# The beginning of an FFN in another order: the forms of x and the first pair's fetch beside the second chunk, a plain unit in front of the first pair

## The chip, the cores and the metric

The kernel runs on one core of a Trainium2 chip. The metric is the device time of one execution in microseconds; it was 1357.7 us, the median of three runs (1357.37 to 1358.7). The engines are PE (TensorE, the matrix products), DVE (VectorE), ACT (ScalarE), POOL (GpSimd) and SP (SyncE, which issues nearly all DMAs). Each engine works through its own instructions in the order in which they were issued, and waits on semaphores for the others.

## The reference

Two layers of a decoder trunk on 256 tokens of width 1024, in float32. Each layer has two gated feed-forward networks (FFNs), a mixer between them and an embedding gate behind them, so there are four FFNs in the program:

```
h = h + 0.5 * SwiGLU_a(RMSNorm(h))
h = h + mixer(RMSNorm(h))
h = h + 0.5 * SwiGLU_b(RMSNorm(h))
h = h + sigmoid(RMSNorm(h) @ W_pg) * (p[i] @ W_pe)
swiglu(x, w1, w3, w2) = (silu(x @ w1) * (x @ w3)) @ w2        # 1024 -> 2816 -> 1024
```

Only the beginning of each FFN is touched by the change, and what is computed stays the same.

## The kernel before

**Products.** Float32 is worked with in two parts: every weight tile and every tile of x is split into a high part (a cast, on ACT, into `whi`, `q` or `xhi`) and the rest (a subtraction, on DVE, into `wlo`, `q` or `xlo`). `mm3` (L102 to L104) forms a product from three matmuls, high by high, high by low, low by high. x holds two token blocks (tb 0 and 1) of 128 tokens, in eight slices (kt) of 128 columns.

**Loads.** `load` (L85 to L87) fetches a tile of 128x1024 (512 KB) into one of four `raw` buffers and splits it. `split_w` splits a tile `wr` that lies in SBUF already (through L135 on ACT and L136 on DVE).

**Chunks, units and pairs.** The hidden width is worked in 11 chunks of 256 columns. Chunk c of w1 and w3 together is four units of 512 KB. A *plain* chunk is 48 matmuls (`up`, or unit by unit `up_unit`, in block lists `("P", c, i)`); `gated` then takes its two banks of PSUM, by `act` on ACT (L236) and `pr` on DVE (L238), to the gated hidden values. `turn` transposes these (L250) for the second product, and `("D", c, j)` is a unit of it, into four banks `acc`. Chunks 5 to 10 are done in *pairs*, by seven products of half size in place of eight (a Winograd form of Strassen's scheme), in the order 1, 2, 5, 3, 6, 7, 4. Each pair fetches four quarters x, y, w and z of the weights, two tiles each (L326), forms sums of them (L330 on DVE; one is an accumulating DMA from POOL, L334), splits them (`make`), and multiplies them with forms of x. Products 1 and 2 use the columns of x as they stand; products 5, 3, 6, 7 and 4 use `q` tiles that `x_forms` makes (L267 to L311): the second token block is rescaled by the quotient of the two row scales, which a matmul with a matrix of ones spreads over the partitions (L274), copied by ACT (L276) and multiplied in by DVE (L297); sums and differences follow (L284, L293, L305), and five splits.

**Order.** The program is written out engine by engine by a tile scheduler that takes the instructions in about the order of the code, and lets an engine's instruction go earlier where its buffers allow. The order around the change is the code's own: chunk 0, chunk 1, then the forms of x, the first pair's fetch, the transposes of chunk 0, and then a block list that starts with "S", a step of the pair: the next `make`, the next sum of quarters, and one product. The first FFN (`first`) differs in what stands beside it: x comes from DRAM in parts, h and the constants are loaded between the units, and chunk 1 goes into the banks `acc`.

The names that the prediction uses: `pr` (L238), the forms' product L274, the adds L293, the scaling L297, the subtractions L284, the last sum L305, the fetch L326, the sum of quarters L330, and the splits by L86/L87 (raw tiles) and L135/L136 (all others).

Of the kernel before, what the change touches and what calls it, by code (L numbers as in the profile page):

```python
# [14 lines left out]
P = 128  # L15
L = 2
S = 256
TB = S // P
D = 1024
# [14 lines left out]
def trunk(ctx: ExitStack, tc: tile.TileContext, a: dict, out: bass.AP):  # L34
# [14 lines left out]
    def const(name, shape):  # L49
        t = cp.tile(shape, F32, tag=name, name=name)  # L50
        tc.keep_in_program_order(nc.sync.dma_start(t, a[name]))
        return t
# [62 lines left out]
    def bank_acc():  # L115
        return bank("acc", 4)
# [74 lines left out]
    def ffn(li, w13, w2, r, g, first=False, aside=None):  # L191
        nonlocal ident
        with tc.tile_pool(name=nm("fp"), bufs=3) as fp:
# [7 lines left out]
            if first:  # L201
                un0 = start(wtile)
            acc = []
            ffT = {}
            prs = {}

            def up(c, un, bank):
                os = []
                for tb in range(TB):
                    o = bank()  # L210
                    for kt in range(KT):
                        w = [x[:, (kt % 2) * 512 : (kt % 2) * 512 + 512] for x in un[kt // 2]]
                        mm3(o, x_at(tb, kt), w, kt == 0, kt == KT - 1)
                        if kt == 1:
                            settle()
                    os.append(o)
                    if r is not None:
                        gated(c, tb, o, r[tb])
                return os


# [12 lines left out]
            def gated(c, tb, o, scale):  # L234
                act = fp.tile([P, FC], F32, tag="act", name=nm("act"), bufs=2)
                A.activation(act, o[:, :FC], AF.Silu, scale=scale)  # L236
                pr = fp.tile([P, FC], F32, tag="pr", name=nm("pr"), bufs=6)
                V.scalar_tensor_tensor(  # L238
                    out=pr, in0=o[:, FC:], scalar=scale, in1=act, op0=ALU.mult, op1=ALU.mult
                )  # L240
                prs[c, tb] = pr
# [189 lines left out]
                        turn(*arg)  # L431
                return following

            for c in range(2):
                if first and c == 1:

                    un = []
                    for i in range(4):
                        un.append(load(w13[li, c, i]))
                        if i < 2:  # L440
                            load_h(i)
                    ident = const("ident", [P, P])
                    r = [norm_r(tb) for tb in range(TB)]
                    for tb, o in enumerate(os0):
                        gated(0, tb, o, r[tb])
                    up(c, un, bank_acc)
                else:
                    os0 = up(c, un0 if first and c == 0 else [load(w13[li, c, i]) for i in range(4)], bank_mm)
                if c == 1:
                    acc.extend(bank_acc() for _ in range(4))  # L450
                    fx = x_forms()
                    wg = pair(5, bank_tr)
                    for q in "xywz":
                        wg[1](q)
                if c >= 1:
                    turn(c - 1)
            wg[0](1)
            if first:
                later()
            wg = block(wg, [  # L460
                ("S",), ("P", 2, 0), ("D", 0, 0), ("S",), ("P", 2, 1), ("S",), ("D", 0, 1), ("P", 2, 2), ("S",),
                ("T", 1), ("P", 2, 3), ("S",), ("D", 1, 0), ("S",), ("D", 1, 1), ("S",), ("T", 2),
            ], (7, bank_tr))
            wg = block(wg, [
# [14 lines left out]
            un = {(c, j): load(w2[li, 2 * c + j]) for c in (9, 10) for j in range(2)}  # L479
# [561 lines left out]
    def load_h(tb):  # L1041
        tc.keep_in_program_order(nc.sync.dma_start(h[tb], a["x"][tb * P : (tb + 1) * P, :]))
# [7 lines left out]
    ident = gmla = gsub = ropec = ropes = lamv = maskm = biasd = masks = tri = None  # L1050
    r = None
# [93 lines left out]
```

## Time and profile before

| | us |
| --- | --- |
| median of three runs | 1357.7 (1357.37 to 1358.7) |
| the profiled execution | 1355.51 |
| its span | 1353.7 |
| its mean granted PE clock | 0.985 of full speed |
| beginnings of the four FFNs (chunk 1 ends) at about | 29, 479, 699, 1150 |

The profiled execution is one execution under the hardware profiler; its rows are given from the span's start, which lies 1.8 us inside the execution. A row of the timeline gives the start, the duration, the engine, the line of the kernel, the operation with output and inputs, and the shape; in brackets stands how long the engine was idle before it and what ended that. Matmuls overlap, so their pace is read from start to start and not from the duration. A row of a window gives, for each engine, the busy time and the number of instructions in that stretch, and behind them the granted clock of PE, the share of the DMA engines' time in use, and their rate.

### The profile page before, as it was taken

What the parts mean: (1) busy time and instruction counts of PE and PEld (TensorE: products, weight loads), DVE (VectorE), ACT (ScalarE), POOL (GpSimd) and SP (SyncE); (2) the same over time, 40 slices, a digit from 0 to 9 for tenths busy, and PEclk for the clock granted to TensorE, in tenths of its full rate; (3) what the DMA queues carried; (4) which work ended last, traced back from release to release, by engine and by line L of the source; (5) the groups of instructions that cost most, each with busy time, mean ns of one, the idle gap of its engine ahead of it and who ended that gap; (6) DMA issues with size and microseconds to landing.
All of it is one profiled execution on the core that took longest, in us unless ns stands there. A gap on an engine that the chain in (4) does not pass through costs nothing.

```text
span 1353.7 us, 18041 instructions
## 1 busy us (share of the span) xinstructions
PE 1308.6 (97%) x6576; PEld 1093.2 (81%) x6576; DVE 1042.0 (77%) x1466; ACT 837.2 (62%) x1257; POOL 69.5 (5%) x133
## 2 busy tenths in 40 slices
PE   8899999999999979999979999999999999799997
PEld 6688889978888858888858888898888788688886
DVE  6998875666768689897769988666666675998875
ACT  5666556665775456665746666566667744666655
POOL 1000000001100000000100000000010000000000
PEclk9899999999999989999999999999999999899999
DMA  8975457433546568555568744473444466675552
GB/s 306 314 251 156 139 164 222 167 125 126 169 143 186 190 211 276 187 147 180 170 219 273 234 121 150 147 225 134 156 145 136 157 187 241 210 236 160 155 169 81
DMA packets 71225, 249.21 MB, mean 184 GB/s; under 512 B 8544, under 2 KB 9184, under 8 KB 71136
## 3 DMA queue, kind: packets, MB, share of 16 engines
q1 hardware_dynamic: 67104, 234.39, 51.1%
q0 software_dynamic: 3456, 12.58, 5.5%
q8 instruction: 51, 0.84, 0.2%
q10 hardware_dynamic: 576, 1.08, 0.2%
q14 instruction: 38, 0.31, 0.1%
HBM read 246.98 MB, written 1.05 MB: 183 GB/s over the span
## 4 chain that ended last, share of the span: by engine, by line
PE 91%; DVE 5%; issue 1%; ACT 1%; DMA 1%; SPq 0%; POOLq 0%; POOL 0%; ACTq 0%
PE mm L102 15%; PE mm L104 14%; PE mm L103 14%; PE acc L103 8%; PE acc L104 8%; PE acc L102 8%; PE tr L103 6%; PE tr L102 5%; PE tr L104 5%; PE tr L250 1%; PE tr L150 1%; DVE q L136 1%; DVE wlo L136 1%; PE tr L742 1%; DVE wlo L87 1%
## 5 line engine op out<-in xcount | busy, mean ns | idle before, releaser
L87 DVE TENSOR_TENSOR wlo<-raw,whi 128x1024 fp32r<-128x1024 f32 (+1 forms) x346 | 411.4, 1200 | 93.1 <-ACT whi L86 90.8
L86 ACT CAST whi<-raw 128x1024 fp32r<-128x1024 f32 (+1 forms) x346 | 354.3, 1033 | 165.7 <-PE acc L104 52.3
L102 PE MATMUL mm<-whi,xhi 128*128 128x512 f32 (+1 forms) x632 | 247.1, 396 | 0.0
L104 PE MATMUL mm<-whi,xlo 128*128 128x512 f32 (+1 forms) x632 | 245.8, 389 | 0.0
L103 PE MATMUL mm<-wlo,xhi 128*128 128x512 f32 (+1 forms) x632 | 245.6, 389 | 0.0
L135 ACT CAST whi<-wr 128x1024 fp32r<-128x1024 f32 (+1 forms) x176 | 179.9, 1032 | 93.2 <-PE acc L104 53.1
L136 DVE TENSOR_TENSOR wlo<-wr,whi 128x1024 fp32r<-128x1024 f32 (+1 forms) x176 | 207.4, 1198 | 25.7 <-ACT whi L135 24.5
L104 PEld LDWEIGHTS mm<-whi,xlo 128*128 128x128 f32 x632 | 118.7, 188 | 24.8 <-DVE xlo L136 0.7
L102 PEld LDWEIGHTS mm<-whi,xhi 128*128 128x128 f32 x632 | 118.7, 188 | 24.4 <-DVE sqk L542 0.7
L104 PE MATMUL acc<-whi,flo 128*128 128x512 f32 x352 | 137.6, 391 | 0.0
L103 PEld LDWEIGHTS mm<-wlo,xhi 128*128 128x128 f32 x632 | 118.9, 188 | 23.1 <-DVE wlo L136 0.2
L103 PE MATMUL acc<-wlo,fhi 128*128 128x512 f32 x352 | 137.1, 390 | 0.0
L102 PE MATMUL acc<-whi,fhi 128*128 128x512 f32 x352 | 135.2, 392 | 0.0
L102 PE MATMUL tr<-whi,q 128*128 128x512 f32 x240 | 94.1, 392 | 0.0
L104 PE MATMUL tr<-whi,q 128*128 128x512 f32 x240 | 93.6, 390 | 0.0
L103 PE MATMUL tr<-wlo,q 128*128 128x512 f32 x240 | 93.4, 389 | 0.0
L330 DVE TENSOR_TENSOR wr<-wr,wr 128x1024 f32<-128x1024 f32 x72 | 86.3, 1222 | 0.0
L104 PEld LDWEIGHTS acc<-whi,flo 128*128 128x128 f32 x352 | 66.1, 188 | 13.8
L103 PEld LDWEIGHTS acc<-wlo,fhi 128*128 128x128 f32 x352 | 66.1, 188 | 13.5
L102 PEld LDWEIGHTS acc<-whi,fhi 128*128 128x128 f32 x352 | 66.1, 188 | 13.4
L102 PE MATMUL tr<-whi,xhi 128*128 128x512 f32 x96 | 42.3, 440 | 33.0 <-ACT whi L135 32.3
L102 PE MATMUL mm<-xhi,whi 128*128 128x256 f32 x256 | 73.8, 288 | 0.0
(253 smaller groups left out, 2169.0 us busy)
## 6 DMA issues: line engine op xcount, KB each, us to landing
wr<-in_w13a SPq DMA_DIRECT2D x48, 512.0 KB, 6.2
raw<-in_wg SPq DMA_DIRECT2D x48, 512.0 KB, 3.8
wr<-in_w13b SPq DMA_DIRECT2D x48, 512.0 KB, 5.8
raw<-in_w2a SPq DMA_DIRECT2D x44, 512.0 KB, 4.4
raw<-in_w2b SPq DMA_DIRECT2D x44, 512.0 KB, 4.3
raw<-in_w13b SPq DMA_DIRECT2D x40, 512.0 KB, 4.3
raw<-in_w13a SPq DMA_DIRECT2D x36, 512.0 KB, 4.6
raw<-in_wqk SPq DMA_DIRECT2D x32, 512.0 KB, 3.8
```

Of the source, the lines that this page charges most:

```text
L86: A.copy(hi[:, c], raw[:, c])
L87: V.tensor_tensor(out=lo[:, c], in0=raw[:, c], in1=hi[:, c].bitcast(F32), op=ALU.subtract)
L102: PE.matmul(o, lhs[0], rhs[0], start=first, stop=False, **more)
L103: PE.matmul(o, lhs[0], rhs[1], start=False, stop=False, **more)
L104: PE.matmul(o, lhs[1], rhs[0], start=False, stop=last, **more)
L135: A.copy(hi, t)
L136: V.tensor_tensor(out=lo, in0=t, in1=hi.bitcast(F32), op=ALU.subtract)
L150: PE.transpose(t[:, j * P : (j + 1) * P], h[tb][:, k * P : (k + 1) * P], ident)
L250: PE.transpose(t[:, j * S + tb * P : j * S + (tb + 1) * P], prs[c, tb][:, j * P : (j + 1) * P], ident)
L330: V.tensor_tensor(out=t[q][u], in0=t[q][u], in1=t[other][u], op=ALU.add)
L742: PE.transpose(t[:, j * P : (j + 1) * P], e[:, j * P : (j + 1) * P], ident)
```

## The change

`up` takes a function that it calls after the first token block. The loop over chunks 0 and 1 is written out: the forms of x (`begin`) are issued ahead of chunk 1's products (in the first FFN between its two token blocks); the first pair's quarters x, y and w are issued between chunk 1's units (in the first FFN behind them), z behind chunk 1; and the first block list begins with the plain unit `("P", 2, 0)` and not with a step of the pair. Because of two added lines, all lines behind `up` have numbers that are two higher: L274 is L276, L293 is L295, L297 is L299, L284 is L286, L305 is L307, L326 is L328, L330 is L332, L238 is L240, L250 is L252.

```diff
-            def up(c, un, bank):
+            def up(c, un, bank, then=None):
                 os = []
                 for tb in range(TB):
...
                     if r is not None:
                         gated(c, tb, o, r[tb])
+                    if tb == 0 and then is not None:
+                        then()
                 return os
...
-            for c in range(2):
-                if first and c == 1:
-
-                    un = []
-                    for i in range(4):
-                        un.append(load(w13[li, c, i]))
-                        if i < 2:
-                            load_h(i)
-                    ident = const("ident", [P, P])
-                    r = [norm_r(tb) for tb in range(TB)]
-                    for tb, o in enumerate(os0):
-                        gated(0, tb, o, r[tb])
-                    up(c, un, bank_acc)
-                else:
-                    os0 = up(c, un0 if first and c == 0 else [load(w13[li, c, i]) for i in range(4)], bank_mm)
-                if c == 1:
-                    acc.extend(bank_acc() for _ in range(4))
-                    fx = x_forms()
-                    wg = pair(5, bank_tr)
-                    for q in "xywz":
-                        wg[1](q)
-                if c >= 1:
-                    turn(c - 1)
+            def begin():
+                nonlocal fx
+                fx = x_forms()
+
+
+            fx = None
+            os0 = up(0, un0 if first else [load(w13[li, 0, i]) for i in range(4)], bank_mm)
+            wg = pair(5, bank_tr)
+            un = []
+            for i in range(4):
+                un.append(load(w13[li, 1, i]))
+                if first and i < 2:
+                    load_h(i)
+                if not first and i > 0:
+                    wg[1]("xyw"[i - 1])
+            if first:
+
+                ident = const("ident", [P, P])
+                r = [norm_r(tb) for tb in range(TB)]
+                for tb, o in enumerate(os0):
+                    gated(0, tb, o, r[tb])
+                for q in "xyw":
+                    wg[1](q)
+                up(1, un, bank_acc, begin)
+            else:
+                begin()
+                up(1, un, bank_mm)
+            wg[1]("z")
+            acc.extend(bank_acc() for _ in range(4))
+            turn(0)
             wg[0](1)
             if first:
                 later()
             wg = block(wg, [
-                ("S",), ("P", 2, 0), ("D", 0, 0), ("S",), ("P", 2, 1), ("S",), ("D", 0, 1), ("P", 2, 2), ("S",),
+                ("P", 2, 0), ("S",), ("D", 0, 0), ("S",), ("P", 2, 1), ("S",), ("D", 0, 1), ("P", 2, 2), ("S",),
                 ("T", 1), ("P", 2, 3), ("S",), ("D", 1, 0), ("S",), ("D", 1, 1), ("S",), ("T", 2),
             ], (7, bank_tr))
```

How it moves instructions is seen at three places. The first is PE in the second FFN, around the end of chunk 1; `mm_4624` is chunk 1's second bank, `tr_4742` product 1's. Before:

```order
L102 MATMUL mm_4624<-whi_4590,xhi 128x512
L103 MATMUL mm_4624<-wlo_4591,xhi 128x512
L104 MATMUL mm_4624<-whi_4590,xlo 128x512
L274 MATMUL tr_4662<-xg_4660,ones 128x128
L250 MATMUL tr_4717<-ident,pr_4540 128x128 x2
L250 MATMUL tr_4717<-ident,pr_4569 128x128 x2
L102 MATMUL tr_4742<-whi_4724,xhi 128x512 [waits Activation_49]
L103 MATMUL tr_4742<-wlo_4725,xhi 128x512 [waits DVE_49]
```

And now, from the end of chunk 1 (`mm_4680`) on, with `mm_4738` and `mm_4739` the banks of the plain unit and `tr_4762` that of product 1:

```order
L104 MATMUL mm_4680<-whi_4602,xlo 128x512
L252 MATMUL tr_4717<-ident,pr_4540 128x128 x2
L252 MATMUL tr_4717<-ident,pr_4569 128x128 x2
L102 MATMUL mm_4738<-whi_4733,xhi 128x512 [waits DVE_49]
L103 MATMUL mm_4738<-wlo_4734,xhi 128x512
L104 MATMUL mm_4738<-whi_4733,xlo 128x512
...
L102 MATMUL tr_4762<-whi_4724,xhi 128x512
L103 MATMUL tr_4762<-wlo_4725,xhi 128x512
L104 MATMUL tr_4762<-whi_4724,xlo 128x512
L102 MATMUL tr_4762<-whi_4724,xhi 128x512
L102 MATMUL mm_4739<-whi_4733,xhi 128x512 [waits DVE_49]
L103 MATMUL mm_4739<-wlo_4734,xhi 128x512
```

The product with the ones has left this place: it now stands ahead of chunk 1's 48 matmuls, as L276. Behind the transposes come the plain unit's matmuls for the first token block, four matmuls of product 1, and then those for the second block, whose bank is freed by a `pr`.

The second place is DVE in the second FFN, from the last split of chunk 1's weights on. Before, the two `pr` of chunk 1 (`pr_4622` and `pr_4651`) stood ahead of the forms:

```order
L238 SCALAR_TENSOR_TENSOR pr_4622<-mm_4595,r_4406,act_4620 128x256
L238 SCALAR_TENSOR_TENSOR pr_4651<-mm_4624,r_4461,act_4649 128x256
L297 TENSOR_TENSOR wr_4666<-wr_4666,rb_4664 128x512 x2
L136 TENSOR_TENSOR flo_4716<-tr_4717,fhi_4715 128x512
L284 TENSOR_TENSOR wr_4668<-wr_4666 128x512
...
L136 TENSOR_TENSOR q_4696<-wr_4666,q_4695 128x512
L136 TENSOR_TENSOR wlo_4725<-wr_4699,whi_4724 128x1024
L136 TENSOR_TENSOR wlo_4729<-wr_4700,whi_4728 128x1024
L136 TENSOR_TENSOR wlo_4733<-wr_4701,whi_4732 128x1024
```

Now, where `pr_4569` belongs to chunk 0 and `pr_4678` and `pr_4707` to chunk 1:

```order
L136 TENSOR_TENSOR wlo_4725<-wr_4571,whi_4724 128x1024
L136 TENSOR_TENSOR wlo_4729<-wr_4572,whi_4728 128x1024
L240 SCALAR_TENSOR_TENSOR pr_4569<-mm_4542,r_4461,act_4567 128x256
L299 TENSOR_TENSOR wr_4618<-wr_4618,rb_4616 128x512 x2
L87 TENSOR_TENSOR wlo_4734<-raw_4732,whi_4733 128x1024
...
L240 SCALAR_TENSOR_TENSOR pr_4678<-mm_4651,r_4406,act_4676 128x256
L307 TENSOR_TENSOR wr_4619<-wr_4619,wr_4620 128x512
L136 TENSOR_TENSOR wlo_4753<-wr_4573,whi_4752 128x1024
...
L136 TENSOR_TENSOR wlo_4757<-wr_4574,whi_4756 128x1024
L240 SCALAR_TENSOR_TENSOR pr_4707<-mm_4680,r_4461,act_4705 128x256
L136 TENSOR_TENSOR flo_4716<-tr_4717,fhi_4715 128x512
```

The splits of quarter x (`wlo_4725`, `wlo_4729`) have moved ahead of chunk 0's second `pr`, and the forms, the splits of y and the plain unit's split now stand between the `pr` of chunk 0 and the last `pr` of chunk 1.

The third place is DVE in the first FFN, from chunk 1's last `pr` on (`pr_372`, which was `pr_316`):

```order
L136 TENSOR_TENSOR wlo_390<-wr_202,whi_389 128x1024
L136 TENSOR_TENSOR wlo_394<-wr_203,whi_393 128x1024
L240 SCALAR_TENSOR_TENSOR pr_301<-acc_274,r_247,act_299 128x256
L240 SCALAR_TENSOR_TENSOR pr_372<-acc_345,r_258,act_370 128x256
L295 TENSOR_TENSOR wr_312<-xhi,xlo 128x512 x2
L299 TENSOR_TENSOR wr_312<-wr_312,rb_310 128x512 x2
L295 TENSOR_TENSOR wr_313<-xhi,xlo 128x512 x2
L286 TENSOR_TENSOR wr_314<-wr_312 128x512
L136 TENSOR_TENSOR flo_381<-tr_382,fhi_380 128x512
L286 TENSOR_TENSOR wr_312<-wr_313,wr_312 128x512
L136 TENSOR_TENSOR q_323<-wr_314,q_322 128x512
L87 TENSOR_TENSOR wlo_419<-raw_417,whi_418 128x1024
```

Here the forms follow chunk 1 as they did before; quarter x is split ahead of them, the four adds L295 have come in from a place far ahead, and the plain unit's split (`wlo_419`) stands behind six of the forms' instructions and `flo`.

## The prediction

> **What bounds the kernel now.** I read the page's first part, then TensorE's waits, then the stretches around the largest of them, then their rows.
>
> ```profile
> span 1353.7 us, 18041 instructions
> PE 1308.6 (97%) x6576; PEld 1093.2 (81%) x6576; DVE 1042.0 (77%) x1466; ACT 837.2 (62%) x1257; POOL 69.5 (5%) x133
> ```
>
> TensorE (PE) is busy for 97% of the span, so an order can win back only the time in which PE stands, or runs at a lower clock. Its waits, grouped (engine, line, releaser: us in total, times, longest):
>
> ```profile
> PE tr L102 <- ACT whi L135: 32.3, 4, 8.1
> PE tr L103 <- DVE wlo L136: 1.9, 4, 0.5
> ```
>
> That is four stalls of 8.1 + 0.5 us, one at each FFN's beginning: 34.2 of the 45.1 us in which PE is not busy. The stretches around the first two (busy us of PE, PEld, DVE, ACT, POOL; granted clock, DMA share, GB/s):
>
> ```profile
> 20.00:30.00 10.00, 8.99 (x41) 6.67 (x39) 4.33 (x9) 4.95 (x12) 1.01 (x3) 1.00 0.61 198
> 30.00:40.00 10.00, 1.60 (x3) 1.00 (x4) 9.89 (x15) 6.33 (x10) 0.00 (x0) 0.66 1.02 396
> 40.00:50.00 10.00, 10.00 (x38) 8.05 (x38) 10.00 (x10) 7.36 (x9) 1.93 (x2) 0.83 0.97 262
> ...
> 460.00:470.00 10.00, 10.00 (x45) 8.28 (x45) 8.32 (x15) 4.93 (x7) 0.05 (x1) 1.00 0.60 178
> 470.00:480.00 10.00, 10.00 (x48) 8.28 (x46) 0.48 (x1) 0.94 (x3) 0.00 (x0) 1.00 1.01 404
> 480.00:490.00 10.00, 1.44 (x4) 0.78 (x3) 9.85 (x15) 6.30 (x12) 0.00 (x0) 0.68 0.36 127
> ```
>
> In the second FFN VectorE (DVE) rests for 9.5 of the ten microseconds before the stall and works for 9.85 of the ten in which PE stands; and the clock falls meanwhile. PE's rows there (start, us, line, operation, idle before and its releaser):
>
> ```profile
> 478.87 0.39 PE L103 MATMUL mm<-wlo,xhi 128*128 128x512 f32 x1
> 479.10 0.40 PE L104 MATMUL mm<-whi,xlo 128*128 128x512 f32 x1
> 479.33 0.39 PE L274 MATMUL tr<-xg,ones 128*128 128x128 f32 x2
> 479.56 0.60 PE L250 MATMUL tr<-ident,pr 128*128 128x128 f32 x4
> 488.24 0.79 PE L102 MATMUL tr<-whi,xhi 128*128 128x512 f32 x1 [8.09 <-ACT whi L135]
> 489.50 0.79 PE L103 MATMUL tr<-wlo,xhi 128*128 128x512 f32 x1 [0.47 <-DVE wlo L136]
> ...
> 493.08 0.63 PE L102 MATMUL tr<-whi,xhi 128*128 128x512 f32 x1
> 493.51 0.59 PE L103 MATMUL tr<-wlo,xhi 128*128 128x512 f32 x1
> 493.93 0.39 PE L104 MATMUL tr<-whi,xlo 128*128 128x512 f32 x1
> ```
>
> L274, the product that the forms of x wait for, stands behind chunk 1, at 479.33. A matmul takes 0.23 us from start to start before the stall and 0.43 us behind it, until 493.93. DVE's rows:
>
> ```profile
> 468.56 0.69 DVE L136 TENSOR_TENSOR pT<-xg,pT 128x512 fp32r<-128x512 f32 x1 [1.28 <-ACT pT L135]
> 469.22 0.48 DVE L238 SCALAR_TENSOR_TENSOR pr<-mm,r,act 128x256 f32<-128x256 f32 x1
> 474.60 0.48 DVE L238 SCALAR_TENSOR_TENSOR pr<-mm,r,act 128x256 f32<-128x256 f32 x1 [4.90 <-ACT act L236]
> 480.04 0.48 DVE L238 SCALAR_TENSOR_TENSOR pr<-mm,r,act 128x256 f32<-128x256 f32 x1 [4.96 <-ACT act L236]
> 480.44 1.28 DVE L297 TENSOR_TENSOR wr<-wr,rb 128x512 f32<-128x512 f32 x2
> ...
> 485.72 2.50 DVE L136 TENSOR_TENSOR q<-wr,q 128x512 fp32r<-128x512 f32 x4
> 488.23 4.63 DVE L136 TENSOR_TENSOR wlo<-wr,whi 128x1024 fp32r<-128x1024 f32 x4
> 492.77 2.36 DVE L330 TENSOR_TENSOR wr<-wr,wr 128x1024 f32<-128x1024 f32 x2
> ```
>
> From 480.44 to 488.23 DVE makes the forms (7.8 us), and only then splits the first pair's quarter x, which product 1 needs. Product 1 uses plain x: it waits for the order alone.
>
> **What the change removes.** L274 (now L276) goes ahead of chunk 1, and in FFNs 2 to 4 the splits of quarter x and most of the forms run while PE works through chunk 1. The cover for 7.8 us of forms and 2.3 us for the two splits of x is the 9.5 us in which DVE rests; what does not fit ends behind chunk 1 and is counted below. What PE wins in FFN 2: from the stall's beginning (488.24 - 8.09 = 480.15) to the return of the clock (493.93) pass 13.78 us, with 11 matmuls in them, worth 11 x 0.2275 = 2.50: 11.3 us. The other FFNs by the same sum:
>
> ```profile
> 37.94 0.80 PE L102 MATMUL tr<-whi,xhi 128*128 128x512 f32 x1 [8.09 <-ACT whi L135]
> 43.51 0.39 PE L104 MATMUL tr<-whi,xlo 128*128 128x512 f32 x1
> ...
> 708.36 0.80 PE L102 MATMUL tr<-whi,xhi 128*128 128x512 f32 x1 [8.08 <-ACT whi L135]
> 712.60 0.39 PE L104 MATMUL tr<-whi,xlo 128*128 128x512 f32 x1
> ...
> 1158.29 0.80 PE L102 MATMUL tr<-whi,xhi 128*128 128x512 f32 x1 [8.08 <-ACT whi L135]
> 1163.05 0.40 PE L102 MATMUL tr<-whi,xhi 128*128 128x512 f32 x1
> ```
>
> FFN 1: 43.51 - 29.85 less 11 matmuls, 11.2. FFN 3: 712.60 - 700.28 less 8, 10.5. FFN 4: 1163.05 - 1150.21 less 9, 10.8. At most, then, 43.8 us.
>
> The Trainium skill (TensorE: Matmul & The Clock Gate, Part 1) says that the array falls to half clock after an idle window of about 3.4 us, and comes back after about as long a busy one, with windows that run freely. By its figure a stall costs at most some 1.7 us of lost clock, an estimate; the rows of FFN 2 give 11.3 - 8.6 = 2.7, FFN 3 only 1.9. FFN 4 gives 2.3. By the page the gain of these three would be some 1.8 us less in sum; the rows decide here.
>
> **What it adds.** The plain unit P 2,0 now comes first, six matmuls for each token block, in two banks that chunk 1 has just used. The second block's matmuls need the bank that the last `pr` (before at 480.04) reads out, and on DVE this `pr` now has the forms ahead of it. I count from the end of chunk 1's last split, 468.56 - 1.28 = 467.3, with 1.15 us for 1024 elements (4.63/4), 0.62 for 512 (2.50/4), 0.45 for a `pr`: two splits of x 2.3; `pr` 0.45; two L299 1.24; the unit's split 1.15; three L286 1.86; an L332 1.15; `pr` 0.45; L307 0.62; two splits of y 2.3; five of q 3.1. That is 14.6 us, so the last `pr` begins at 481.9 and ends at 482.4. PE comes to this place at about 479.3 + 0.2 (transposes) + 6 x 0.2275 + 4 x 0.2275 (product 1's first) = 481.8. A wait of 0.6 us if nothing lands late. Below stands nothing, above two splits that wait for their data, 2.5. I take 0.9, since chunk 1's last unit now stands behind quarters on the queue. Behind the waiting matmul stand eight of product 1, the rest of whose operands are ready, and nothing on another engine needs them sooner.
>
> DVE keeps pace afterwards: before, it has done all that stands up to L330 x2 and the unit's split at 492.77 + 2.3 + 1.15 = 496.2. Now it has all of that behind it at 482.4 + 0.62 (flo) + 1.15 + 0.62 (pT, moved back) = 484.8, 11.4 us earlier; PE's lead is 10.4.
>
> FFNs 2 to 4: 11.3 + 10.5 + 10.8 - 3 x 0.9 = 29.9.
>
> **The fetch.** A tile of 512 KB takes 1.3 us at 404 GB/s. SP issues the quarters like this before:
>
> ```profile
> 467.30 0.33 SPq L85 DMA_DIRECT2D raw<-in_w2b  x1
> 467.81 18.96 SPq L326 DMA_DIRECT2D wr<-in_w13b  x10
> ```
>
> In FFNs 2 and 4 x and y go between chunk 1's first and second unit and w ahead of its fourth: six tiles, 7.8 us, in stretches whose DMA share is 0.60 and less. In FFN 3 they stay behind chunk 1. I cost this at nothing beyond the 0.9; without that cover the fourth unit's matmuls start up to 7.8 us late, less what the raw buffers had in hand.
>
> **FFN 1 is different.** DVE works without a break from the stall on, and beyond it:
>
> ```profile
> 14.92 0.69 DVE L293 TENSOR_TENSOR wr<-xhi,xlo 128x512 f32<-128x512 f32 x1
> 29.74 0.48 DVE L238 SCALAR_TENSOR_TENSOR pr<-acc,r,act 128x256 f32<-128x256 f32 x1 [1.56 <-ACT act L236]
> ...
> 83.00:93.00 10.00, 10.00 (x45) 8.04 (x44) 10.00 (x11) 6.49 (x9) 1.37 (x2) 1.00 0.85 209
> 93.00:103.00 10.00, 10.00 (x48) 8.27 (x47) 9.88 (x11) 6.12 (x8) 0.00 (x0) 1.00 0.80 256
> 103.00:113.00 10.00, 10.00 (x48) 8.27 (x47) 7.29 (x8) 6.54 (x9) 0.00 (x0) 1.00 0.74 272
> ```
>
> The change takes two splits of x (2.3) out of the busy stretch and puts into it the four adds L293 (now L295), which ran at 10 to 17 us, in DVE's slack: 4 x 0.62 = 2.5. Also an L330 (1.15) goes behind the pair's last sum. So DVE is about 1 us earlier, with some slack of PE's unknown: 1.5, from -1 (the unit's split waits behind six forms) to 11.2 (DVE was not the bound).
>
> Sum: 29.9 + 1.5 = 31.4. The profiled execution took 1355.5 us (span 1353.7), 2.2 below the median of 1357.7. 1355.5 - 31.4 = 1324.1, as a median **1326**.
>
> **Rivals.**
> *FFN 1 wins too.* If PE's splits there have slack on DVE, all four gain: 43.8 - 4 x 0.9 = 40.2, 1317. For it: the clock falls there just the same. Against: DVE's 9.89 and 10.00 of ten.
> *DVE becomes the bound everywhere.* Each FFN then gains what FFN 1 does, 1.5: 6 us, 1352; with half of DVE's rest used (4.7 of 9.5 in three FFNs, and 1.5) 1342. For it: DVE is at 9.85 behind the stall. Against: its 0.48 of ten ahead of it.
> *The stall only changes place.* P 2,0 waits in front of the banks as long as product 1 did: 1358. Against: by the sum above the last `pr` ends at 482.4, not at 488.
> *Chunk 1 starves.* Place: SP's queue in FFNs 2 and 4, where chunk 1's last three units stand behind x's first tile, which waits for a buffer of the mixer. If that came free only at 467.8, the fourth unit would be ninth in line: 467.8 + 9 x 1.3 + 2.3 (its splits) = 481.8, then 30 matmuls 6.8 and 2 us of clock: 490.6, and with P 2,0 and product 1 about where PE was before. Each microsecond later costs two in sum, against 11.1 of FFNs 3 and 1: it decides from 6 us later, 474. Held till 478, the sum is 2 x 10 - 11 = 9 us slower, 1367. For it: SP takes its work in order. Against: the same fetch went at 467.81 with 0.5 us behind the issue ahead of it, so its buffers were free by then.
> The Trainium skill (DMA: Bandwidth & Descriptors, the anatomy of one DMA) states that a semaphore is waited for on the issuing sequencer and the DMA engines just consume their queues; by that a held quarter does hold the units behind it. No row here shows a quarter that was held.
>
> **How the numbers follow.** Forecast 0.65; FFN 1 too 0.15; DVE bound 0.10; place 0.03; starved 0.07. The likeliest's own range is 1319 (no new wait, FFN 1 with 6) to 1334 (2.5 each, FFN 1 with -1). The whole range goes down to 1314 (43.8 in full) and up to 1343, half of DVE's rest. A change under 0.2% (2.7 us) can't be told from none here. Faster 0.65 + 0.15 + 0.10 = 0.90, same 0.03, slower 0.07.
>
> **What would show it.** After: PE's four waits for whi L135 gone in FFNs 2 to 4, in their place one under 2.5 us for a `pr`; DVE's busy time in the ten microseconds ahead of chunk 1's end above 8 instead of 0.48; the clock at 1.00 there; FFN 1 with PE waiting several microseconds for the unit's split or later operands. Wrong would be: a wait inside chunk 1 for `whi` L86 (starved), or FFNs 2 to 4 with less than 8 us each (DVE).

## The result and the profile after

The changed kernel takes 1318.97 us, the median of three runs (1318.01 to 1319.56), against 1357.7 before: a ratio of 0.9712 with a 95% interval of 0.969 to 0.9734, or 38.7 us. The forecast was 1326 with a range from 1314 to 1343. The profiled execution has a span of 1316.9 us against 1353.7, so 36.8 us are to be found in the traces.

The first part of the page after, and the grouped waits of TensorE (us in total, times, longest):

```profile
span 1316.9 us, 18057 instructions
PE 1301.2 (99%) x6576; PEld 1087.1 (83%) x6576; DVE 1039.6 (79%) x1466; ACT 835.9 (63%) x1257; POOL 66.5 (5%) x133
...
PE mm L102 <- ACT whi L86: 3.7, 1, 3.7
...
PE tr L102 <- DVE m L358: 0.5, 1, 0.5
```

The four waits of 8.1 us are gone. The largest that is left, 3.7 us, is in the first FFN. PE's busy time fell by 7.4 us with as many matmuls in it: fewer of them run at half clock (the mean granted clock is 0.997 in place of 0.985).

The stretches after, at the places that were quoted before:

```profile
30.00:40.00 10.00, 6.31 (x22) 4.49 (x21) 10.00 (x16) 7.08 (x10) 0.00 (x0) 0.83 0.79 249
40.00:50.00 10.00, 8.38 (x35) 6.07 (x34) 10.00 (x10) 6.35 (x9) 1.93 (x2) 1.00 0.98 301
...
460.00:470.00 10.00, 10.00 (x47) 8.31 (x46) 9.42 (x13) 6.41 (x10) 0.00 (x0) 1.00 0.76 269
470.00:480.00 10.00, 9.97 (x46) 7.91 (x45) 10.00 (x16) 7.30 (x11) 0.93 (x1) 1.00 0.83 209
```

Between 470 and 480 VectorE is busy for 10.00 us, where it was for 0.48; PE is busy for 10.00 and 9.97 us and has the full clock in both stretches of the second FFN. In the first FFN the hole is smaller but still there: PE busy 6.31 of ten, clock 0.83 (before: 1.60, 0.66).

How much each FFN gained is read from the same instruction in both traces, the addition to `h` at the end of its second product on VectorE (start, us). Before:

```profile
198.03 0.68 DVE L486 SCALAR_TENSOR_TENSOR h<-acc,h 128x512 f32<-128x512 f32 x1
648.80 0.69 DVE L486 SCALAR_TENSOR_TENSOR h<-acc,h 128x512 f32<-128x512 f32 x1
868.10 0.69 DVE L486 SCALAR_TENSOR_TENSOR h<-acc,h 128x512 f32<-128x512 f32 x1
1318.65 0.68 DVE L486 SCALAR_TENSOR_TENSOR h<-acc,h 128x512 f32<-128x512 f32 x1
```

After, where the same line is nine further down:

```profile
193.82 0.68 DVE L495 SCALAR_TENSOR_TENSOR h<-acc,h 128x512 f32<-128x512 f32 x1
633.27 0.68 DVE L495 SCALAR_TENSOR_TENSOR h<-acc,h 128x512 f32<-128x512 f32 x1
842.73 0.68 DVE L495 SCALAR_TENSOR_TENSOR h<-acc,h 128x512 f32<-128x512 f32 x1
1281.84 0.68 DVE L495 SCALAR_TENSOR_TENSOR h<-acc,h 128x512 f32<-128x512 f32 x1
```

The lead is 4.21, 15.53, 25.37 and 36.81 us. By FFN that is 4.2, 11.3, 9.8 and 11.4; what lies between the FFNs is contained in these differences. The forecast was 1.5, 10.4, 9.6 and 9.9.

What became of the stall is seen on PE in the second FFN after, around the end of chunk 1 (475.11 is its last matmul):

```profile
475.11 0.39 PE L104 MATMUL mm<-whi,xlo 128*128 128x512 f32 x1
475.34 0.60 PE L252 MATMUL tr<-ident,pr 128*128 128x128 f32 x4
475.70 0.48 PE L102 MATMUL mm<-whi,xhi 128*128 128x512 f32 x1
...
477.86 0.39 PE L102 MATMUL tr<-whi,xhi 128*128 128x512 f32 x1
478.28 0.50 PE L102 MATMUL mm<-whi,xhi 128*128 128x512 f32 x1
```

and on VectorE there, from the second split of quarter x (464.66) to the last `pr` (477.75):

```profile
464.66 1.22 DVE L136 TENSOR_TENSOR wlo<-wr,whi 128x1024 fp32r<-128x1024 f32 x1 [0.48 <-ACT whi L135]
...
474.20 2.49 DVE L136 TENSOR_TENSOR q<-wr,q 128x512 fp32r<-128x512 f32 x4
...
477.75 0.48 DVE L240 SCALAR_TENSOR_TENSOR pr<-mm,r,act 128x256 f32<-128x256 f32 x1
```

The last form is split at 476.69, not at 488.22 as before, and the matmul that has to follow the last `pr` starts at 478.28, as that `pr` ends (478.23). PE loses about 0.2 us there: matmuls start 0.42 apart in place of 0.23.

### The profile page after: what moved, and what is told of

Its sections match the earlier page's. It is cut to its first block, busy times and chain, and to the rows that moved or that the text cites. A ratio compares the mean times of both kernels' runs of the same rounds, so it can differ in the third digit from the quotient of the medians.

```text
span 1316.9 us, 18057 instructions
## 1 busy us (share of the span) xinstructions
PE 1301.2 (99%) x6576; PEld 1087.1 (83%) x6576; DVE 1039.6 (79%) x1466; ACT 835.9 (63%) x1257; POOL 66.5 (5%) x133
## 3 DMA queue, kind: packets, MB, share of 16 engines
HBM read 246.98 MB, written 1.05 MB: 188 GB/s over the span
## 4 chain that ended last, share of the span: by engine, by line
PE 96%; DVE 3%; ACT 1%; issue 0%; DMA 0%; POOLq 0%; POOL 0%; ACTq 0%
PE mm L102 15%; PE mm L104 15%; PE mm L103 15%; PE acc L103 8%; PE acc L104 8%; PE acc L102 8%; PE tr L102 6%; PE tr L104 6%; PE tr L103 6%; PE tr L252 1%; PE tr L150 1%; PE tr L751 1%; PE acc L853 1%; PE acc L835 1%; PE acc L725 1%; PE tr L714 1%
## 5 line engine op out<-in xcount | busy, mean ns | idle before, releaser
L87 DVE TENSOR_TENSOR wlo<-raw,whi 128x1024 fp32r<-128x1024 f32 (+1 forms) x346 | 411.6, 1200 | 94.8 <-ACT whi L86 90.2
L86 ACT CAST whi<-raw 128x1024 fp32r<-128x1024 f32 (+1 forms) x346 | 354.6, 1032 | 155.0 <-PE acc L104 50.2
L135 ACT CAST whi<-wr 128x1024 fp32r<-128x1024 f32 (+1 forms) x176 | 181.3, 1033 | 114.3 <-PE acc L104 54.8
L136 DVE TENSOR_TENSOR wlo<-wr,whi 128x1024 fp32r<-128x1024 f32 (+1 forms) x176 | 208.3, 1196 | 28.2 <-ACT whi L135 26.7
L332 DVE TENSOR_TENSOR wr<-wr,wr 128x1024 f32<-128x1024 f32 x72 | 86.2, 1219 | 0.0
L103 PEld LDWEIGHTS acc<-wlo,fhi 128*128 128x128 f32 x352 | 66.1, 188 | 14.6 <-DVE wlo L87 1.0
L104 PE MATMUL mm<-xhi,wlo 128*128 128x256 f32 x256 | 72.5, 283 | 0.0
```

The costliest lines, as they stand in the source:

```text
L86: A.copy(hi[:, c], raw[:, c])
L87: V.tensor_tensor(out=lo[:, c], in0=raw[:, c], in1=hi[:, c].bitcast(F32), op=ALU.subtract)
L103: PE.matmul(o, lhs[0], rhs[1], start=False, stop=False, **more)
L104: PE.matmul(o, lhs[1], rhs[0], start=False, stop=last, **more)
L135: A.copy(hi, t)
L136: V.tensor_tensor(out=lo, in0=t, in1=hi.bitcast(F32), op=ALU.subtract)
```

## The experiments

Theory A is the prediction's: the stall was a matter of order on VectorE and ScalarE, where the forms stood in front of the splits of quarter x. By it the parts of the change need not add up, since any that puts the splits in front of the stall removes it. Its rivals give each part a share of its own. For the first FFN, whose gain was three times the forecast, there are three more: VectorE alone bounds it; ScalarE's order does (the unit's cast stands behind another); or, theory C, GpSimd was held up before by VectorE's early adds.

All runs in one table. The gain by FFN is read as above, in the profiled execution (for the fourth FFN up to the first block's addition, which gives 0.3 us less than the lead at the very end). It is one execution of each kernel: the two executions of the changed kernel differ by 1.3 in the second FFN, and those of the kernel with fetch and unit by 1.0 in the third. Ratios are against runs of the kernel before on the same chip.

| kernel | median us | ratio (95%) | gain of FFN 1, 2, 3, 4 |
| --- | --- | --- | --- |
| changed kernel | 1318.97 | 0.9712 (0.969 to 0.9734) | 4.2, 11.3, 9.8, 11.2 |
| the same, once more | 1319.67 | 0.9729 (0.9716 to 0.9742) | 4.2, 10.0, 9.8, 11.1 |
| forms only | 1320.78 | 0.9734 (0.9719 to 0.9748) | 3.6, 10.2, 10.6, 10.4 |
| fetch only | 1322.89 | 0.9752 (0.9734 to 0.977) | 2.6, 10.9, 8.1, 10.2 |
| unit only | 1356.74 | 1.0002 (0.999 to 1.0014) | 0.6, 0.3, 0.1, 0.1 |
| forms and fetch | 1321.84 | 0.9744 (0.9726 to 0.9763) | 3.1, 11.6, 10.1, 11.2 |
| fetch and unit | 1318.04 | 0.9718 (0.9705 to 0.9731) | 4.9, 11.7, 10.2, 11.1 |
| fetch and unit, once more | 1318.85 | 0.9728 (0.9715 to 0.9741) | 4.5, 11.6, 9.2, 11.1 |
| change, adds early again | 1320.81 | 0.9735 (0.972 to 0.9749) | 3.0, 10.4, 9.6, 11.2 |
| change, adds behind chunk 0 | 1323.09 | 0.9752 (0.9737 to 0.9766) | 1.3, 10.4, 9.6, 11.2 |
| change, six sums left out | 1317.28 | 0.9711 (0.9695 to 0.9727) | 5.9, 11.3, 9.8, 11.0 |
| before, adds behind chunk 0 | 1354.68 | 0.9986 (0.9976 to 0.9995) | 0.7, -0.3, -0.2, -0.1 |
| change, adds and cast moved | 1320.72 | 0.9739 (0.9725 to 0.9752) | 4.4, 11.2, 9.8, 11.1 |

### Each part alone

**The forms alone:** `begin` ahead of chunk 1, with the fetch and the block list as before.

```diff
-            wg = pair(5, bank_tr)
...
-                if not first and i > 0:
-                    wg[1]("xyw"[i - 1])
...
-            wg[1]("z")
...
+            wg = pair(5, bank_tr)
+            for q in "xywz":
+                wg[1](q)
...
-                ("P", 2, 0), ("S",), ("D", 0, 0),
+                ("S",), ("P", 2, 0), ("D", 0, 0),
```

> Of the three parts of the change, only the forms of x go ahead of chunk 1; the first pair's quarters are fetched behind chunk 1, and the first block begins with product 1, as before. Theory A (the stall was the order alone; any part that puts DVE's work into its 9.5 idle us ahead of chunk 1's end removes it, so the parts overlap and do not add): the forms run in DVE's idle time, quarter x is split behind them and still ahead of chunk 1's end, FFNs 2 to 4 gain 9 to 11 us each, FFN 1 up to 3: 1323 to 1329. Theory B (the parts add up, a third of 38.7 each): about 1345. In the trace A wants the PE wait for whi L135 under 2 us in FFNs 2 to 4.

**The fetch alone:** the forms behind chunk 1 as before, and the block list begins with "S".

```diff
-                up(1, un, bank_acc, begin)
+                up(1, un, bank_acc)
...
-                begin()
...
+            begin()
...
-                ("P", 2, 0), ("S",), ("D", 0, 0),
+                ("S",), ("P", 2, 0), ("D", 0, 0),
```

> Only the fetch of quarters x, y and w goes beside chunk 1; the forms come behind chunk 1 and the block begins with product 1, as before. Theory A: the splits of x and y and the sums of quarters run in DVE's idle time, so products 1 and 2, the plain unit and the first down unit (48 matmuls, 11 us) cover the 8 to 9 us of the forms behind chunk 1; FFNs 2 to 4 gain 8 to 11 each: 1322 to 1332. Theory B: about 1345. A also wants DVE busy over 5 of the ten us before chunk 1's end.

**The unit alone:** forms and fetch behind chunk 1 as before, and the block list begins with the plain unit.

```diff
-            wg = pair(5, bank_tr)
...
-                if not first and i > 0:
-                    wg[1]("xyw"[i - 1])
...
-                up(1, un, bank_acc, begin)
+                up(1, un, bank_acc)
...
+            begin()
+            wg = pair(5, bank_tr)
+            for q in "xywz":
+                wg[1](q)
```

> Only the plain unit comes first in the block; forms and fetch as before. Theory A: on DVE the forms and the splits of x still stand ahead of the unit's split, so PE waits for that split as long as it waited for product 1 (8 us and more): no change, 1355 to 1361. Theory B: about 1345.

**Forms and fetch, without the unit:** only the block list is put back.

```diff
-                ("P", 2, 0), ("S",), ("D", 0, 0),
+                ("S",), ("P", 2, 0), ("D", 0, 0),
```

> The whole change but for the plain unit: the forms and the fetch beside chunk 1, the block begins with product 1. Theory A: nothing left for the unit to cover in FFNs 2 to 4, so within 1 us of the changed kernel there; in FFN 1 product 1 came first anyway. 1318 to 1321. Theory B: about 1332.

The forms alone gain 34.8 us in sum, the fetch alone 31.8, both together 36.0: they do not add. By the medians it is 35.8, 33.7 and 34.7, and the interval of the forms alone overlaps both of the changed kernel's. (The forms alone came out 2 us better than was expected, forms and fetch 0.8 worse; a third of the gain for each part would have been some 1345.) The unit alone gains nothing that can be measured. How two different edits remove the same stall is read from VectorE in the second FFN. With the forms alone, the forms' last splits and then the quarter's:

```profile
471.62 2.50 DVE L136 TENSOR_TENSOR q<-wr,q 128x512 fp32r<-128x512 f32 x4
474.04 0.48 DVE L240 SCALAR_TENSOR_TENSOR pr<-mm,r,act 128x256 f32<-128x256 f32 x1
474.50 3.50 DVE L136 TENSOR_TENSOR wlo<-wr,whi 128x1024 fp32r<-128x1024 f32 x3
477.91 0.48 DVE L240 SCALAR_TENSOR_TENSOR pr<-mm,r,act 128x256 f32<-128x256 f32 x1
```

With the fetch alone, the second split of quarter x, and the forms only behind the last `pr`:

```profile
466.90 1.23 DVE L136 TENSOR_TENSOR wlo<-wr,whi 128x1024 fp32r<-128x1024 f32 x1 [1.19 <-ACT whi L135]
...
477.70 0.48 DVE L240 SCALAR_TENSOR_TENSOR pr<-mm,r,act 128x256 f32<-128x256 f32 x1
478.10 1.28 DVE L299 TENSOR_TENSOR wr<-wr,rb 128x512 f32<-128x512 f32 x2
```

Product 1 needs the splits of quarter x, and not the forms. In the first kernel these splits follow on forms that are done ahead of the last `pr`; in the second they pass the forms, which then run under product 1 and the units behind it. What the fetch alone lacks is seen on PE: it waits for the plain unit's split, which stands among the forms, 3.4 us in FFNs 2 to 4 together; with the unit in front as well this is 0.3 and 1.4 us in the two executions further down. With the unit alone, PE's great waits are what they were before:

```profile
PE tr L102 <- ACT whi L135: 32.3, 4, 8.1
```

PE reaches product 1 ahead of the unit there all the same: on VectorE the unit's split stands behind the forms and the first two splits of the quarters. So that run does not show what the unit would bring if PE really came to it first. The rest is theory A, shown by runs. It also corrects how the prediction put the parts together: it did not divide the gain between forms and fetch, and the fetch stands in its sum only as a cost, put at nothing; by itself the fetch brings nearly as much as the forms.

**Fetch and unit, without the forms:** `begin` goes behind chunk 1 again, and all else stays as in the change. It was run twice.

```diff
-                up(1, un, bank_acc, begin)
+                up(1, un, bank_acc)
...
-                begin()
...
+            begin()
```

> The changed kernel with the forms of x issued behind chunk 1 again (the fetch beside chunk 1 and the plain unit first remain). Theory A (parts overlap): the forms are covered by the plain unit, products 1 and 2 and the down unit, so within 4 us of the changed kernel: 1318 to 1323. Theory B (parts add up): 13 us above it, 1332.

> Fetch beside chunk 1 and the plain unit first, the forms behind chunk 1, once more with more rounds, to see whether it is at least as fast as the full change. If moving the forms is worth nothing once the other two parts are there, its ratio to the kernel before lies at 0.971 to 0.973, where the full change's two measurements lie (0.9712 and 0.9729); in the profile PE waits for no pr in FFN 2, since on DVE no forms stand ahead of chunk 1's last pr.

0.9718 and 0.9728, against 0.9712 and 0.9729 for the changed kernel: the intervals overlap nearly whole. Once fetch and unit are there, moving the forms is worth nothing that these runs can tell. The part that the prediction names first, the forms' move, is one that can be left out. The one part that no run leaves out by itself is the fetch, with forms and unit in place.

### The new wait

**The changed kernel again**, with no edit, beside two others on one chip.

> The changed kernel once more, beside the other two on one chip: 1318 to 1320.

In this execution the second FFN gained 1.3 us less, and the wait that was predicted stands there (PE, VectorE and ScalarE in the second FFN):

```profile
479.58 0.50 PE L102 MATMUL mm<-whi,xhi 128*128 128x512 f32 x1 [1.05 <-DVE pr L240]
...
465.96 1.23 DVE L136 TENSOR_TENSOR wlo<-wr,whi 128x1024 fp32r<-128x1024 f32 x1 [1.51 <-ACT whi L135]
...
464.36 0.62 ACT L135 CAST pT<-xg 128x512 fp32r<-128x512 f32 x1 [1.33 <-DMA xg<-in_pT]
```

In the first profile of this kernel the same cast was:

```profile
463.06 0.62 ACT L135 CAST pT<-xg 128x512 fp32r<-128x512 f32 x1 [0.30 <-DMA xg<-in_pT]
```

The tile `pT` landed 5.4 us after its issue and not 4.4. Its cast stands on ScalarE ahead of the second cast of quarter x; so VectorE's split waited 1.51 in place of 0.48 us, and the last `pr` came at 479.05 and not at 477.75. A transfer that belongs to the next stage decides the wait. Four of the kernels below have the same order on VectorE in the second FFN: where `pT` took 4.1 and 4.6 us to land, PE waited for the `pr` not at all and 0.2 us, and the FFN gained 11.3 and 11.2; where it took 5.2 and 5.4, PE waited 0.7 and 1.0 us, and the FFN gained 10.4.

### The first FFN

VectorE took less time there than was counted. From the last `pr` of chunk 1 to the end of the pair's last sum, before and after (window, its length, then busy time of PE, PEld, DVE, ACT, POOL):

```profile
29.74:83.23 53.49, 44.94 (x192) 36.39 (x190) 52.02 (x62) 35.97 (x46) 2.52 (x3) 0.90 0.89 308
```

```profile
28.77:78.95 50.18, 44.87 (x190) 35.01 (x188) 49.91 (x59) 33.59 (x43) 1.93 (x2) 0.97 0.89 291
```

It begins 0.97 us earlier and is 3.31 shorter: 4.3 in sum, the gain of 4.2. Of the 3.31, VectorE's busy time gives 2.1 (52.02 to 49.91) and its idle time 1.2 (1.47 to 0.27). The prediction had about 1.0 of busy time, and 0.5 for what it did not know. Four small operations of the next stage that were in the stretch before and no longer are make up some 0.5 of the busy time.

The 0.97 at the beginning comes, as the next two runs show, from the adds of the forms, which before ran at 10 to 17 us, in what was taken for slack. GpSimd has a small operation at that time in a row that ends in the scale `r` for `act` and `pr`. Before:

```profile
15.22 3.32 POOL L171 TENSOR_SCALAR ss<-ss 128x1 f32<-128x1 f32 x1 [14.26 <-ACT junk L164]
```

After:

```profile
15.12 0.31 POOL L171 TENSOR_SCALAR ss<-ss 128x1 f32<-128x1 f32 x1 [14.16 <-ACT junk L164]
```

**Theory C alone, in the kernel before:** only the first FFN's four adds (L293) are put behind the second `pr` of chunk 0 on VectorE.

```diff
-                V.scalar_tensor_tensor(
+                last[c, tb] = V.scalar_tensor_tensor(
...
-                    V.tensor_tensor(
+                    i = V.tensor_tensor(
...
+                    if first:
+                        behind(i, last[0, 1])
```

> The kernel before the change, with nothing else changed than that FFN 1's four adds run behind chunk 0's second pr (into DVE's idle 2.1 and 1.6 us there) and no longer at 10 to 17 us. Theory C: POOL's L171 takes 0.5 us or less in place of 3.32, the first pr comes 2 to 3 us earlier, chunk 1 ends about 1 us earlier, and the time falls by about 1 us. Rival: L171 still takes 1.5 us or more, nothing gained.

```profile
15.46 0.32 POOL L171 TENSOR_SCALAR ss<-ss 128x1 f32<-128x1 f32 x1 [14.50 <-ACT junk L164]
...
18.24 0.48 DVE L239 SCALAR_TENSOR_TENSOR pr<-mm,r,act 128x256 f32<-128x256 f32 x1
```

The operation takes 0.32 us in place of 3.32, the first `pr` comes at 18.24 in place of 20.08, the last at 28.50 in place of 29.74. What lies between is seen in chunk 1 of the kernel before:

```profile
22.40 0.50 PE L102 MATMUL acc<-whi,xhi 128*128 128x512 f32 x1 [0.35 <-ACT whi L86]
23.88 0.50 PE L103 MATMUL acc<-wlo,xhi 128*128 128x512 f32 x1 [0.51 <-DVE wlo L87]
```

On ScalarE the casts of these units stand behind `act`, which waits for `r`, 2.75 us before and 0.17 here. Both waits of PE are gone here, and in the changed kernel. The first FFN gains 0.7 in this execution, but the later FFNs lose it again (0.1 is left at the end). The ratio of the medians is 0.9986 (0.9976 to 0.9995), 2 us and just apart from one, where about 1 us was expected. The unit alone, too, shows 0.6 in the first FFN, so a size of 0.7 from one execution is rough.

**The reverse, in the changed kernel:** the adds are made by a function of their own, `x_adds`, that is called ahead of chunk 1.

```diff
+            def x_adds():
...
-            def x_forms():
+            def x_forms(made=None):
...
-                fx = x_forms()
+                fx = x_forms(made)
...
+                made = x_adds()
```

> The changed kernel, but in FFN 1 the four adds of the forms are issued ahead of chunk 1 and run in DVE's early slack at 10 to 17 us, as they did before the change. Theory C (FFN 1's extra gain came in part from POOL: in the old kernel its L171, a 128x1 operation, took 3.32 us while DVE worked back to back on the adds and splits, and 0.31 us in the changed one): L171 takes 1.5 us or more again and the first pr comes over 1 us later. The busy stretch of DVE behind chunk 1 is 2.5 us shorter at the same time, so the time is within 2 us of the changed kernel, 1317 to 1321. Rival: POOL's long operation had another cause, L171 stays at 0.3 us and the time falls by up to 2.5 us, to 1316.5.

```profile
15.95 1.47 POOL L171 TENSOR_SCALAR ss<-ss 128x1 f32<-128x1 f32 x1 [14.98 <-ACT junk L164]
17.52 1.34 POOL L173 TENSOR_SCALAR ms<-ss,ss 128x1 f32<-128x1 f32 x1
```

L173 takes 0.26 us in the changed kernel. The first `pr` is at 20.04 (17.90), the last of chunk 1 at 29.95 (28.77), and PE's two waits in chunk 1 are back, with 0.32 and 0.51 us. The first FFN gains 3.0 where the change gains 4.2, though VectorE has 2.5 us less to do behind chunk 1. Not all of this is C's: on ScalarE the unit's cast now stands behind all five casts of the forms and not behind one, at 37.12 in place of 34.03, and PE's wait for it is 5.6 us in place of 3.7. (FFN 2 lost 0.9: there `pT` took 5.4 us to land.) The two runs together show C at the end of chunk 1, where it is 1.24 and 1.18 us; how much of that reaches the FFN's end is 0.7 in one execution, and was not separated in the other.

**The adds further ahead:** as in the last kernel, but ordered behind chunk 0's second `pr`.

```diff
+                made = x_adds()
+                for i in made[1]:
+                    behind(i, last[0])
```

> The changed kernel, but in FFN 1 the four adds run on DVE directly behind chunk 0's second pr, in front of chunk 1's end; the plain unit's load also goes ahead of the quarters on SP. Theory D (FFN 1 is bound by DVE's work behind chunk 1, which is 2.5 us shorter here, with POOL undisturbed): 1 to 2.5 us below the changed kernel, 1316.5 to 1318. Rival: FFN 1 is bound by the fetch (DMA share 0.98 there): no gain or a loss, since the quarters land later, 1319 to 1322.

The first FFN gained only 1.3. The scheduler had moved the loads too: on SP three raw tiles go ahead of the quarters. The last two of them and the quarters on SP's queue in this kernel:

```profile
18.18 0.33 SPq L85 DMA_DIRECT2D raw<-in_w2a  x1
21.36 0.33 SPq L85 DMA_DIRECT2D raw<-in_w13a  x1
21.73 3.94 SPq L335 DMA_DIRECT2D wr<-in_w13a  x8
```

In the changed kernel six of these eight tiles were issued from 11.84 us on. PE now waits for whi L135, 4.2 us in two waits. With 1323.09 us it lies beyond both expected ranges. The run therefore says nothing on where the adds are best; the FFN is some 3 us worse with a late fetch, though the adds were moved in the same run.

**VectorE's work taken away:** the first pair of the first FFN without its three sums of quarters, six tiles of L332, 6.9 us on VectorE.

```diff
                 def add(q, other):
+                    if first and c == 5:
+                        return
```

> The changed kernel without the six sums of quarters on DVE in FFN 1's first pair (6 x 1.15 = 6.9 us of DVE's work; the products of that pair are therefore others than the kernel needs). Theory D: FFN 1 is bound by DVE, so 3 to 7 us are gained there: 1312 to 1316. Rival (the order of PE or the fetch bounds it): under 1 us, 1318 to 1319.

The FFN gains 5.9 against 4.2: of 6.9 us taken from VectorE, 1.7 come through. PE's wait for whi L86 stays at 3.7 us. The time lies between the two expected ranges. So VectorE's load alone does not bound this FFN's beginning, and it is not without a part in it.

**Both together:** the adds go between the splits of quarter x and chunk 1's `pr`, and with that the unit's cast goes ahead of a form's cast on ScalarE.

```diff
+                if first and c == 1 and tb == 0:
+                    behind(last[0], made[1][-1])
...
+                made = x_adds()
+                for i in made[1]:
+                    behind(i, last[0])
```

> The changed kernel with FFN 1 in another order only: on DVE the four adds run behind the splits of quarter x and ahead of chunk 1's two pr, POOL undisturbed and the loads on SP in the changed kernel's order; on ACT the plain unit's cast comes ahead of the forms' first cast, for which PE waited 3.7 us. Theory D2 (in FFN 1 DVE's work and PE's wait for that cast bound each other within about 2 us): both are shortened, 1 to 2 us are gained: 1317 to 1318. Rival (one bound remains as it was): no change, 1318.5 to 1319.5.

What it was meant to cure, in the changed kernel (PE, then ScalarE):

```profile
35.12 1.22 PE L102 MATMUL mm<-whi,xhi 128*128 128x512 f32 x2 [3.69 <-ACT whi L86]
...
33.50 0.62 ACT L135 CAST q<-wr 128x512 fp32r<-128x512 f32 x1 [1.45 <-DVE wr L286]
34.03 1.04 ACT L86 CAST whi<-raw 128x1024 fp32r<-128x1024 f32 x1
```

The unit's cast, 1.04 us, waits behind a cast that waits for VectorE. And PE with the cast moved:

```profile
32.68 0.73 PE L102 MATMUL mm<-whi,xhi 128*128 128x512 f32 x2 [1.62 <-ACT whi L86]
...
44.00 0.50 PE L103 MATMUL acc<-wlo,fhi 128*128 128x512 f32 x1 [1.80 <-DVE wlo L87]
```

The wait fell from 3.69 to 1.62, one of 0.73 for whi L135 stayed, and a new one of 1.80 came behind them, on VectorE. The FFN gains 4.4 against 4.2 in the profiled execution; the median of the four runs (1318.71 to 1323.3) is 1320.72, which neither theory had expected. The wait had only changed place. None of these kernels can be told to be better than the changed one.

## Why the prediction was right, and where not

**The bound.** Right: four stalls, and an order could win them back; the forms and the fetch each did so alone. PE's busy share rose from 97 to 99%.

**What is removed in FFNs 2 to 4** was put at 11.3, 10.5 and 10.8 with the lost clock in it. Measured, with any new wait in it: 11.3, 9.8 and 11.2 (11.4 at the very end). Here the sum with the clock from the rows held. The stalls alone, 8.56 in each, would have given 25.7; these three FFNs gained 32.3 to 32.6. In the third, 0.3 of the 0.7 that are missing is a wait for `m` (L358) inside the pair, 0.52 us where it was 0.23; the rest was not traced.

The Trainium skill (TensorE: Matmul & The Clock Gate, Part 1) would have had this 1.8 us smaller in sum; that is 30.8, where the rows gave 32.6 ahead of any deduction. Measured are 32.3 to 32.6, and 31.0 in the second execution with a wait of 1.05 in it; this case speaks for the rows.

**The new wait**, 0.9 in each of three FFNs, was too dear. The step that failed is its size: 0.6 was worked out, 0.9 was taken, and 0.2 came. With the 4.2 us that the first FFN had gained taken off, the count put the last `pr` at 477.7 and PE at 477.6; they came at 477.75 and 478.1 (where matmul 478.28 would have stood without a pause, 477.86 + 0.23). So the count of 14.6 us on VectorE was right to a few tenths, and PE came 0.5 later than counted; in the second execution the wait was 1.05. In the third and fourth FFN neither execution lists a wait for a `pr`. In sum over three FFNs that is 0.2 to 1.1 us, not 2.7.

**Chunk 1 starves** had its price from a held tile. No wait inside chunk 1 for a raw tile shows in the waits after: the 3.7 us of whi L86 are at 35.12, behind chunk 1 of the first FFN. *DVE everywhere* fell with the FFNs' gains above 9 us, and *the stall only changes place* with the rows around 478.

**FFN 1** is the term that was mis-sized: 1.5 forecast, 4.2 measured in both profiles. Its step, that VectorE sets the end there, was half right: when VectorE had 4.3 us less to do or to wait, the FFN was 4.2 shorter, but with 6.9 us more of its work taken away only 1.7 more were won. What failed is the bookkeeping. The four adds were costed at 2.5 us in a busy stretch and at nothing where they had stood; where they had stood they held up GpSimd, and without them the stretch began 0.97 earlier. And VectorE's own idle time in the stretch, 1.47 us, and small work of the next stage in it weren't looked at. How the 4.2 divide among these was not separated run by run. The rival *FFN 1 wins too* (11.2 at most) is half true: PE's waits went from 8.56 to 5.2 us (3.69 + 0.85 + 0.63, rows below), and part of the clock came back.

```profile
44.62 0.51 PE L102 MATMUL tr<-whi,q 128*128 128x512 f32 x1 [0.85 <-ACT whi L135]
45.75 0.50 PE L103 MATMUL acc<-wlo,fhi 128*128 128x512 f32 x1 [0.63 <-DVE wlo L87]
```

**The signs named.** PE's four waits gone: yes. One under 2.5 us for a `pr` in their place: 1.05 in the second execution, 0.2 in the first. VectorE above 8 of ten ahead of chunk 1's end (475.3): yes, 9.42 from 460 to 470 and 10.00 from 470 to 480. Clock at 1.00 there: yes. The first FFN with a wait of several microseconds for the unit's split: yes, 3.69, by its cast.

**The sum.** 36.8 in the span against 31.4: 2.7 too little in the first FFN, 2.4 to 2.7 in the others, most of it the wait that hardly came. A second gap of some 2 us is between profile and medians: before, the profiled execution was 2.2 below its median, after it was the median itself.

## What to carry to other kernels

When a product stalls at a stage's beginning, look at what the engine that feeds it did in the ten microseconds ahead: 0.48 busy ahead of the stall and 9.85 in it was the sign here that an order could win it back. One edit that put the needed operand in front was then nearly enough, so each further one should be tried without the others. Price such a stall from its beginning to the return of the full pace, not by the wait alone. And work that is moved out of a stretch called slack should be looked at there too, on every engine that ran beside it.

## What the runs showed of the hardware that was not expected

**GpSimd held for ten times its duration.** An operation on 128x1 elements took 3.32 us before and 0.31 after. VectorE's rows before, at that time:

```profile
15.52 1.23 DVE L87 TENSOR_TENSOR wlo<-raw,whi 128x1024 fp32r<-128x1024 f32 x1
16.66 0.70 DVE L293 TENSOR_TENSOR wr<-xhi,xlo 128x512 f32<-128x512 f32 x1
17.26 1.23 DVE L87 TENSOR_TENSOR wlo<-raw,whi 128x1024 fp32r<-128x1024 f32 x1
```

Three operations that follow on one another without a gap end at 18.49, and the GpSimd operation ends at 18.54. With the adds elsewhere, VectorE pauses behind its first one, and GpSimd is through at once: all ten traces without the early adds have 0.23 to 0.32 there, the four with them, the kernel before among these, 1.47 to 3.32. In the run with the adds early again L171 ends at 17.42 and L173 at 18.86, where VectorE's operations in two unbroken stretches end at 17.36 and 18.81.

The Trainium skill (SBUF — State Buffer, "SBUF: two separate sides") says that a VectorE operation with two inputs in SBUF and a GpSimd operation that reads SBUF lock a pair of ports against each other, and that the loser is blocked for the whole instruction. The rows agree, and go further: the loser was held over three in a row. Whether the two inputs are what does it wasn't tried, but the changed kernel's trace has a case that fits: at 665.71 an L173 took 1.48 us while VectorE ran an L87 and an L136 with two inputs in SBUF, up to 667.06; it ended at 667.19, beside an L154 (666.97 to 667.66) that takes `tr` from PSUM.

**A wait of 1.80 us can cost the full clock, too.** In the last kernel PE stood for 1.80 us up to 44.00; the stretch from 46 to 48 then ran at half clock (window, its length, PE, PEld, DVE, ACT, POOL busy, granted clock, DMA share, GB/s):

```profile
46.00:48.00 2.00, 2.00 (x6) 1.57 (x5) 2.00 (x3) 1.68 (x2) 0.00 (x0) 0.50 1.00 260
```

In the changed kernel waits of 0.85 and 0.63 us, a microsecond apart, left it at 1.00. The clock fell some 1.3 us after the work had begun again, and was back by 48.9; behind the waits of 1.62 and 0.73 in the same kernel it was at 0.66 from 35 to 40. At half clock from 45.26 to 48.91 some 1.8 us are lost (an estimate: half of that time), so it can be why that kernel's shorter waits (4.2 against 5.2 us) gave only 0.2 us; this was not separated.

The Trainium skill (TensorE: Matmul & The Clock Gate, Part 1) names an idle window of about 3.4 us for this; here a wait of about half that was enough. What decides it wasn't tried.
